# Attention of one decoder step: turns in row halves, other products in 32-column tiles, sample parts added on TensorE, PSUM banks given out freely, a new order

## The chip, the cores and the metric

The kernel runs on one core of one Trainium2 chip. The metric is device time in microseconds (us), median of the runs. One execution is profiled; its span reaches from the first to the last instruction. Engines: TensorE (PE in the profile; PEld is its weight loads), VectorE (DVE), ScalarE (ACT), GpSimd (POOL), and SyncE (SP), which issues nearly all DMAs.

## The reference, cut to what matters

One step of a two-layer decoder for 256 prompt tokens and 8 sample sequences of 4 new tokens each (past 2048), in fp32. Layer 0 is a short convolution, layer 1 is sparse attention; each stands between two half-step SwiGLU FFNs. The change lies in the attention of layer 1 alone. It has 16 heads of 64 (4 key/value heads), and adds three branches:

```
def nsa_attend(q, t_pos, gates, k_cmp, v_cmp, gather_sel, kv_win, s_win):
    s_c = einsum(q, k_cmp) * scale;  p_c = softmax(where(m_c, s_c, NEG)) * m_c;  o_c = einsum(p_c, v_cmp)
    imp = p_c.sum(group).reshape(..., nb_s, ratio).sum(-1)
    score = where(forced, FORCE_BONUS, where(valid, imp, -FORCE_BONUS))
    _, idx = lax.top_k(score, min(TOP_N, nb_s))
    k_sel, v_sel = gather_sel(idx);  p_s = softmax(masked q.k_sel);  o_s = einsum(p_s, v_sel)
    p_w = softmax(masked q.k_win);   o_w = einsum(p_w, v_win)
    return gates[0] * o_c + gates[1] * o_s + gates[2] * o_w
```

## The kernel before, in words

The FFNs and projections are streams of fp32r products, 128x128 weights against 288 token columns. They lie before and behind the attention and the change leaves them alone.

The attention is the function `nsa`. Its last part lays down every piece of work as a step (`step`, a `Task`) with an engine, a duration from the table `TAKES`, the steps it comes after, the buffers it takes (`Slot`, in rings of `RINGS`) and a rank. `Plan.run` lists the steps: of those that can start first it takes the one of the lowest rank, and emits its instructions at once, so the order of each engine's queue is that list. The ranks are the numbers in `CHUNKS`, `HEADS`, `TAILS`, `UNITS` and `COMPRESSED`, found by a search outside the program. `MODES` names the shape in which a step uses TensorE's array ("f" 128x128, "p" 128x64, "c" 128x32 in four column tiles, "h" 64x128 in two row tiles), and the planner counts `SWITCH` for each change of it.

The steps are:

- Samples, `sequences(i)`, four pairs of sequences (32 query rows each for two key/value head pairs, 128 partitions). A head: `small` (scores against compressed and new keys), `max`, `parts` (exp), `share`, `rank`, `best` (the top 16 blocks). Then five chunks of 512 keys, one of the window ("w") and four of the pages: `S` (scores), `top` (mask and maximum, DVE), `exp` (ACT), `turn` (four transposes of 128x128), `copy` (PSUM to SBUF, ACT), `V` (values), and for the first four `og` (the chunk's output to `Og`, ACT). Each chunk has its own maximum, so the parts must be weighted before they are added. The tail: `min`, `wg`, `wg2` (weights `w`), `turn_s`, `copy_s`, `V_s` (the small part), `sum`, `add`, `last`, `own` (weighted sum of the parts and a mask on DVE, into the tile rB or rms), `out` (a product with the 0/1 matrix `Sel` that puts each row in its place) and `oh_s`, `ol_s`.
- Prompt, `prompt_unit(u)`, eight units: `s0`, `s1` (scores of the later and the earlier half of the queries), `t0`, `t1` (DVE) and `e0`, `e1` (ACT), `factor`, `f1`, `f0` (scaling, DVE), three `pturn` of four transposes each, three copies (two on ACT, one on DVE, into PA and PB), `p_v` (ten products), `oh`, `ol`.
- Pages come in through SP: 40 sets of 1 MB, in a fixed order. A set's load is issued by `load_pages` when a `V` step has freed a buffer; the weights of the next stage come behind the last set. Three weight splits (`whi` on ACT, `wlo` on DVE) have the highest ranks and so fill what is left.

PSUM has eight banks of 512 fp32 columns: before, a ring of four ("mm", the scores), one of two ("tr", turns), and one of two ("acc", values and small products).

Of the kernel before, what the change touches and what calls it, by code (L numbers as in the profile page):

```python
# [8 lines left out]
F32 = mybir.dt.float32  # L9
# [44 lines left out]
RINGS = dict(mm=4, tr=2, acc=2, U=2, PA=1, PB=1, S=3, PTs=2, small=2, pc=1, score=1, mk=2, sum=2, PTm=2)  # L54
TAKES = dict(
    small=0.4, max=0.55, parts=0.9, share=0.44, rank=0.21, best=1.5, S=0.87, S2=1.0, top=0.61, top_w=0.89, exp=0.71, turn=0.47, copy=0.5,
    copy_v=0.6, V=0.9, og=0.16, min=0.25, wg=0.38, wg2=1.6, turn_s=0.15, copy_s=0.21, sum=1.57, V_s=0.3, add=0.28, last=0.36, own=0.29,
    out=0.25, oh_s=0.12, ol_s=0.14, cmp=1.34, cmp_e=0.32, cmp_n=2.0, cmp_t=0.28, cmp_c=0.34, s0=0.95, s1=0.54, t0=0.34, t1=0.21, e0=0.49,
    e1=0.385, factor=0.39, f0=1.13, f1=0.6, pturn=0.47, p_v=1.95, oh=0.28, ol=0.34, whi=0.96, wlo_v=1.15, cs=1.2, cs_c=0.5, cs_t=0.5,
# [5 lines left out]
MODES = dict(turn="f", pturn="f", rank="f", turn_s="f", out="f", cmp_t="f", cs="c", cs_t="f", p_v="fp",  # L65
             S="c", V="c", small="c", V_s="c", s0="h", s1="h")
SWITCH = 0.12


NEAR, STAY = 0.129, 56.5102  # L70
CHUNKS = ((964.53, 896.1799), (1327.2414, 995.6261), (1417.341, 1380.5317), (1478.0066, 997.9328),
# [4 lines left out]
HEADS = (952.1558, 1031.7885, 1431.353, 1421.0384)  # L76
TAILS = (1410.3538, 1473.7793, 1457.1762, 926.1094)
UNITS = ((1408.4431, 1368.5397), (1437.9733, 959.7242), (1297.9535, 1272.967), (1420.513, 1500.4049),
    (1413.2876, 1393.186), (1364.7109, 1016.3831), (1045.6014, 1472.1569), (1020.1863, 1529.1656))
COMPRESSED = (1332.6098, 1463.1332)  # L80
SHARED = ("cmp_n", "sum", "share", "own", "wg2", "wlo_v")
# [68 lines left out]
class Plan:  # L150
# [3 lines left out]
    def __init__(self, rings):  # L154
        self.rings = {n: [None] * k for n, k in rings.items()}
        self.free, self.tasks, self.mode, self.port = {}, [], None, (0.0, 0.0)

    def add(self, *a, **k):
        t = Task(*a, **k)
        self.tasks.append(t)  # L160
        return t

    def start(self, t):
# [8 lines left out]
        taken = {}  # L172
        for s in t.slots:
            n = taken[s.ring] = taken.get(s.ring, -1) + 1
            last = self.rings[s.ring][n]
            for x in last.users if last else ():
                if x.end is None:
                    return None
                at = max(at, x.end + (0.0 if x.engine == t.engine else HOP[x.engine]))
        return at  # L180

    def run(self):
        left = list(self.tasks)
        while left:
# [5 lines left out]
            left.remove(t)  # L190
            for s in t.slots:
                self.rings[s.ring] = self.rings[s.ring][1:] + [s]
# [133 lines left out]
def tile_step(ctx, tc, x_turned, state_turned, cmp_pages, sel_pages, cache_win, win_pages, page_table,  # L326
# [9 lines left out]
    banks = {}  # L336

    @contextmanager
    def psum_banks(**counts):
        with tc.tile_pool(name="psum", bufs=2, space=PSUM) as pool:  # L340
            banks.update(pool=pool, **counts)
            yield

    def bank(name):
        return banks["pool"].tile([P, 512], F32, name=name, bufs=banks[name])
# [7 lines left out]
    def accb():  # L353
        return bank("acc")

# [34 lines left out]
    def tr(out, in_):  # L390
        k = in_.shape[0]
        nc.tensor.transpose(out, in_, ident[:k, :k])  # L392

# [509 lines left out]
    def nsa(at):  # L903
# [20 lines left out]
        G, Sel, okvg, okp, vmask = [A(n, [P, w]) for n, w in (("G", P), ("Sel", 64), ("okvg", 16), ("okp", 2), ("vmask", 16))]  # L924
# [39 lines left out]
        put(ts, Sel, lin[:, :64], col["csel"], None, op0=OP.is_equal)  # L964
        put(ts, okvg, lin[:, :16], col["kvg"], None, op0=OP.is_equal)
        put(ts, okp, lin[:, :2], col["kp"], None, op0=OP.is_equal)

# [252 lines left out]


# [51 lines left out]
        cs, cS, turned_ = Slot("acc"), Slot("S"), Slot("tr")  # L1273
# [20 lines left out]
        def cmp_turn():  # L1294
            units["ct"] = trb()
            for a in range(2):
                tr(units["ct"][:, a * P:(a + 1) * P], s[:, a].rearrange("p h n -> p (h n)"))
# [8 lines left out]
        x = Slot("tr")  # L1306
        c4 = step("PE", "cmp_t", cmp_turn, [c3], [x], rank=r)
        cmp_done = step("DVE", "cmp_c", lambda: nc.vector.tensor_copy(PcT, units.pop("ct")[:, :NP]), [c4], uses=[x], rank=r)

        def prompt_unit(u, pr, g):  # L1310

            t, (rs, r) = {}, UNITS[u]
            sl = {n: Slot(n) for n in ("U", "PA", "PB", "acc")}
# [29 lines left out]
            for half in range(2):  # L1343
                banks_ = [Slot("mm"), Slot("mm")]
# [26 lines left out]
            def turn(n):  # L1371
                src_ = (t["S0"], t["S1"][:, :, :P], t["S1"][:, :, P:])[n]
                t["tr", n] = trb()
                for j in range(4):
                    tr(t["tr", n][:, j * P:(j + 1) * P], src_[:, j])

            def put(n):
                if n == 0:
                    t["PA"] = T("PA", [P, 4, NP], F32, RINGS["PA"])
                if n == 2:  # L1380
                    t["PB"] = T("PB", [P, 4, P], F32, RINGS["PB"])
                dst = t["PA"][:, :, n * P:(n + 1) * P] if n < 2 else t["PB"]
                v = t.pop(("tr", n)).rearrange("p (j q) -> p j q", j=4)
                if n == 1:
                    nc.vector.tensor_copy(dst, v)  # L1385
                else:
                    nc.scalar.activation(dst, v, AF.Copy)

            puts = []
            for n in range(3):  # L1390
                x = Slot("tr")
                p = step("PE", "pturn", lambda n=n: turn(n), [(f0, f1, f1)[n]], [x], [sl["U"]], r - 0.2)
                puts.append(step("DVE" if n == 1 else "ACT", "copy_v" if n == 1 else "copy", lambda n=n: put(n), [p] + puts[:1],
                                 {0: [sl["PA"]], 2: [sl["PB"]]}.get(n, []), [x] + [sl["PA"]] * (n == 1), r - 0.2))

            def values():
                o = t["o"] = accb()
                mm(o[:, :NP], VcBig[:, u], PcT, True, False)
                for br in range(2):
                    for a, pt in ((0, t["PA"]), (1, t["PB"])):  # L1400
                        for kp in range(2):
                            vs = V[br + 1][:, a, (2 * pr + kp) * HD:(2 * pr + kp + 1) * HD]
# [358 lines left out]
```

## Time and profile before

| | us |
|---|---|
| median of 3 runs (lowest, highest) | 1186.28 (1185.25, 1186.79) |
| the profiled execution | 1186.15 |
| its span | 1184.1 |
| PE, DVE, ACT, POOL busy over the span | 1172.9, 749.5, 579.8, 171.9 |

The profiled execution lies 2.05 us above its span (what comes before the first and after the last instruction) and 0.13 us below the median. The granted TensorE clock is 0.998 of full speed. Times in the rows below are us from the start of the span; the attention's planned steps run from about 843.5 to 946.8. In the rows, `tr<-ident,S` is a turn, `mm<-...,Qbd` a chunk's scores, `acc<-...,PTs` its values, `mm<-kT,qT` a unit's scores, `acc<-ss,VcBig`, `acc<-PA,V` and `acc<-PB,V` a unit's values. An fp32 product stands there as two instructions, a transpose as one. Instructions that run side by side in tiles of the array overlap in time.

### The profile page before, as it was taken

How to read it: one execution, taken by the hardware profiler on the slowest of the kernel's cores; microseconds unless marked ns; L12 is line 12 of the kernel's file. 1: busy time of each engine (PE TensorE's matmuls, PEld its weight loads, DVE VectorE, ACT ScalarE, POOL GpSimd, SP SyncE). 2: the span in 40 equal slices, each digit the busy share in tenths (PEclk: the TensorE clock that was granted, in tenths of full speed). 3: DMA queues.
4: the chain of work that ended last, by engine and by line, in shares of the span. 5: the costliest groups of instructions: out<-in, count | busy, mean ns of one | idle time of the engine just before them, and what ended most of it. 6: DMA issues, size and time to landing. Idle time of an engine off the chain costs nothing. (4 is left out here: it accounts for less than half of the span.)

```text
span 1184.1 us, 25826 instructions
## 1 busy us (share of the span) xinstructions
PE 1172.9 (99%) x10034; PEld 1114.9 (94%) x10034; DVE 749.5 (63%) x1407; ACT 579.8 (49%) x1013; POOL 171.9 (15%) x221
## 2 busy tenths in 40 slices
PE   9999999999999999999999999999999999999997
PEld 9999999999999999999999999999766799999997
DVE  7663665667766455466564566687688876655654
ACT  6543444534644344445443444544468755434444
POOL 1160111223311100112110011130000021100111
PEclk9999999999999999999999999999999999999999
DMA  7864764766637477467663553597999647765531
GB/s 302 302 206 156 272 196 159 270 212 234 228 134 280 144 241 273 144 191 245 208 230 107 196 196 108 193 367 276 321 374 383 222 162 280 257 224 197 184 114 61
DMA packets 89468, 262.02 MB, mean 221 GB/s; under 512 B 9826, under 2 KB 42979, under 8 KB 74115
## 3 DMA queue, kind: packets, MB, share of 16 engines
q1 hardware_dynamic: 88466, 249.71, 60.2%
q0 software_dynamic: 256, 8.32, 1.9%
q10 hardware_dynamic: 624, 2.34, 0.5%
q8 instruction: 80, 1.31, 0.4%
q14 instruction: 42, 0.34, 0.1%
HBM read 257.31 MB, written 11.35 MB: 227 GB/s over the span
## 5 line engine op out<-in xcount | busy, mean ns | idle before, releaser
L301 DVE TENSOR_TENSOR wlo<-raw,whi 128x1024 fp32r<-128x1024 f32 (+3 forms) x363 | 418.0, 1158 | 229.3 <-ACT whi L291 228.0
L291 ACT ACTIVATE whi<-raw 128x1024 fp32r<-128x1024 f32 (+3 forms) x366 | 345.5, 953 | 191.8 <-PE mm L362 184.4
L362 PE MATMUL mm<-xh,whi 128*128 128x288 f32 x1456 | 419.3, 290 | 0.0
L362 PE MATMUL mm<-xh,wlo 128*128 128x288 f32 x1456 | 416.0, 288 | 0.3 <-DVE wlo L301 0.3
L362 PE MATMUL mm<-xl,whi 128*128 128x288 f32 x1456 | 416.1, 288 | 0.0
L362 PEld LDWEIGHTS mm<-xh,whi 128*128 128x128 f32 x1456 | 271.3, 187 | 1.3 <-issue 0.3
L362 PEld LDWEIGHTS mm<-xh,wlo 128*128 128x128 f32 x1456 | 271.0, 187 | 0.5 <-DVE wlo L301 0.5
L362 PEld LDWEIGHTS mm<-xl,whi 128*128 128x128 f32 x1456 | 271.1, 187 | 0.2
L362 PE MATMUL mm<-Ah,whi 128*128 128x288 f32 x768 | 222.6, 290 | 0.0
L362 PE MATMUL mm<-Al,whi 128*128 128x288 f32 x768 | 221.5, 288 | 0.0
L362 PE MATMUL mm<-Ah,wlo 128*128 128x288 f32 x768 | 221.4, 288 | 0.0
L362 PEld LDWEIGHTS mm<-Ah,whi 128*128 128x128 f32 x768 | 143.7, 187 | 0.5 <-issue 0.4
L362 PEld LDWEIGHTS mm<-Al,whi 128*128 128x128 f32 x768 | 143.8, 187 | 0.0
L362 PEld LDWEIGHTS mm<-Ah,wlo 128*128 128x128 f32 x768 | 143.7, 187 | 0.0
L610 POOL TENSOR_TENSOR a<-s,t 128x288 f32<-128x288 f32 x80 | 66.6, 832 | 520.0 <-DVE t L608 420.5
L606 ACT ACTIVATE s<-t 128x288 f32<-128x288 f32 x88 | 39.0, 444 | 135.4 <-DVE t L604 135.1
L362 PE MATMUL mm<-zh,whi 128*128 128x288 f32 x352 | 101.6, 289 | 0.0
L362 PE MATMUL mm<-zh,wlo 128*128 128x288 f32 x352 | 101.4, 288 | 0.0
L362 PE MATMUL mm<-zl,whi 128*128 128x288 f32 x352 | 101.4, 288 | 0.0
L362 PEld LDWEIGHTS mm<-zl,whi 128*128 128x128 f32 x352 | 65.8, 187 | 0.1
L362 PEld LDWEIGHTS mm<-zh,whi 128*128 128x128 f32 x352 | 65.8, 187 | 0.1
L362 PEld LDWEIGHTS mm<-zh,wlo 128*128 128x128 f32 x352 | 65.8, 187 | 0.0
(314 smaller groups left out, 1096.7 us busy)
## 6 DMA issues: line engine op xcount, KB each, us to landing
raw<-in_w_ffb_gu_dram SPq DMA_DIRECT2D x44, 1024.0 KB, 5.0
raw<-in_w_ffa_gu_dram SPq DMA_DIRECT2D x42, 1024.0 KB, 5.1
cp<-in_cmp_pages_dram SPq DMA_DIRECT2D x256, 128.0 KB, 4.4
early<-in_sel_pages_dram SPq DMA_DIRECT2D x64, 256.0 KB, 5.3
raw<-in_w_ffa_down_dram SPq DMA_DIRECT2D x16, 768.0 KB, 4.2
raw<-in_w_conv_in_dram SPq DMA_DIRECT2D x12, 1024.0 KB, 4.8
raw<-in_w_ffb_down_dram SPq DMA_DIRECT2D x16, 768.0 KB, 4.2
raw<-in_w_ffa_down_dram SPq DMA_DIRECT2D x16, 640.0 KB, 4.0
```

The lines of the kernel that those rows point to most:

```text
L291: self.nc.scalar.activation(parts[0], v, AF.Copy)
L301: (lower or self.nc.vector).tensor_sub(parts[1], v, parts[0])
L362: nc.tensor.matmul(out, lhsT, rhs, start=start, stop=stop, skip_group_check=True)
L606: nc.scalar.activation(s1, t1, AF.Silu)
L610: (nc.vector if last else nc.gpsimd).tensor_mul(a, s1, t2)
```

## The change

1. Turns. `turn`, `pturn` and the turn of the compressed part transpose the upper and lower 64 rows of a block apart (`halves_turned`): each half moves 64 columns instead of 128, in its own row tile of the array and into its own PSUM bank, so a turn holds two banks. The two later `pturn` of a unit become one step, `pturn2`. The tile PT replaces PA and PB.
2. All other products of the plan go in four 32-column tiles (`quarters`): `p_v` (before one 128x128 and eight 128x64 products), `rank`, `out`, and `turn_s`, now a product with the identity. Only one turn (`cs_t`) keeps the 128x128 shape.
3. The samples' parts. `sum`, `add`, `last` and `own` go. `sel` on DVE makes five weighted copies of `Sel` (128x128 each), the small and the last part are copied out of PSUM, and `out` adds six products in PSUM. The products that keep the array at work ahead of the last `out` go from five to three.
4. PSUM is one tile of eight banks. Within the plan, a step takes the banks that come free first; outside it the old three rings are kept.
5. The copies `copy`, `og` and the two new ones go to ACT or DVE by a string of 68 letters, `MOVES`: 49 A, 19 D.
6. New entries in `TAKES`, and new ranks. `STAY` is 3183 (before 56.5): among steps that could start at the same time, one of the array's present shape always goes first.

The core of the diff:

```diff
-RINGS = dict(mm=4, tr=2, acc=2, U=2, PA=1, PB=1, S=3, PTs=2, small=2, pc=1, score=1, mk=2, sum=2, PTm=2)
+RINGS = dict(bank=8, U=2, PT=1, S=3, PTs=2, small=2, pc=1, score=1, mk=2, sum=2, PTm=1, sel=1, last=1)
...
-MODES = dict(turn="f", pturn="f", rank="f", turn_s="f", out="f", cmp_t="f", cs="c", cs_t="f", p_v="fp",
+MODES = dict(turn="h", pturn="h", pturn2="h", rank="c", turn_s="c", out="c", cmp_t="h", cs="c", cs_t="f", p_v="c",
              S="c", V="c", small="c", V_s="c", s0="h", s1="h")
...
+MOVES = "ADDDAAAAAADADAAADDDAAAADADAAAAAAAAAAAAAAAAADDAAAAADDDDAAAAAAAADDAADA"
...
+    def places(self, t):
+        taken = {}
+        for s in t.slots:
+            ring, used = self.rings[s.ring], taken.setdefault(s.ring, [])
+            if s.ring == "bank":
+                used.append(min((self.clear(x, t.engine), n) for n, x in enumerate(ring) if n not in used)[1])
+            else:
+                used.append(len(used))
+        return taken
...
+    def both_banks():
+        a, b = sorted(planned[0].given)
+        return banks[0][:, a:b + 1:b - a]
...
+    def halves_turned(out, in_):
+        for h in range(2):
+            r = slice(h * 64, (h + 1) * 64)
+            nc.tensor.transpose(out[:, h], in_[r], ident[r, r])
+
+    def quarters(out, lhsT, rhs, start=True, stop=True):
+        for q in range(4):
+            c = slice(q * 32, (q + 1) * 32)
+            mm(out[c], lhsT[:, c], rhs, start, stop)
...
                 def turn(d=d):
-                    d["pt"] = trb()
+                    d["pt"] = both_banks()[:, :, :256].rearrange("p h (s x) -> p h s x", s=4)
                     for s in range(4):
-                        tr(d["pt"][:, s * P:(s + 1) * P], d["S"][:, s])
+                        halves_turned(d["pt"][:, :, s], d["S"][:, s])
...
+            def chosen():
+                t["sel"] = [space(k // 2)[:, k % 2 * P:(k % 2 + 1) * P] for k in range(5)]
+                for k in range(5):
+                    ts(t["sel"][k].rearrange("p (h c) -> p h c", h=2), Sel, t["w"][:, 2 + k:3 + k], None, op0=OP.mult)
...
-            def sums():
-                ...
-                ts(a, Og[:, 0], w[:, 2:3], None, op0=OP.mult)
-                for n in range(3):
-                    stt(a, Og[:, 1 + n], w[:, 4 + n:5 + n], a, op0=OP.mult, op1=OP.add)
...
             def turn_out():
                 left_out.append(i)
+                t["o"] = accb()
                 if len(left_out) == 4:
-                    fillers(5)
-                t["o"] = accb()
-                mm(t["o"][:, :64], t["a"], Sel, True, True)
+                    for _ in range(3):
+                        quarters(t["o"][:, P:2 * P], ones, ones)
+                parts_ = [(t["Og"][:, k], t["sel"][k].rearrange("p (h c) -> p h c", h=2)) for k in range(4)]
+                parts_ += [(t["s"], Sel), (t["last"], t["sel"][4].rearrange("p (h c) -> p h c", h=2))]
+                for n, (v, w) in enumerate(parts_):
+                    for q in range(4):
+                        c = slice(q * 32, (q + 1) * 32)
+                        mm(t["o"][c, :64], v[:, c], w[:, q // 2], n == 0, n == 5)
```

More of the change, by code (lines that the diff above doesn't have):

```diff
@@ L50 @@
 WAITS = (24, 3, 4, 9)
-RINGS = dict(mm=4, tr=2, acc=2, U=2, PA=1, PB=1, S=3, PTs=2, small=2, pc=1, score=1, mk=2, sum=2, PTm=2)
+RINGS = dict(bank=8, U=2, PT=1, S=3, PTs=2, small=2, pc=1, score=1, mk=2, sum=2, PTm=1, sel=1, last=1)
 TAKES = dict(
[L56 to L59, printed above, removed]
+    small=0.4, max=0.55, parts=0.9, share=0.44, rank=0.16, best=1.5, S=0.86, S2=1.0, top=0.61, top_w=0.89, exp=0.71, turn=0.25, copy=0.5,
+    copy_v=0.6, og_v=0.2, V=0.875, og=0.16, min=0.25, wg=0.38, wg2=1.6, turn_s=0.22, copy_s=0.21, V_s=0.3, sel=0.68, out=0.75, oh_s=0.12, ol_s=0.14, cmp=1.34, cmp_e=0.32, cmp_n=2.0, cmp_t=0.13, cmp_c=0.34, s0=0.92, s1=0.5, t0=0.34, t1=0.21, e0=0.49,
+    e1=0.385, factor=0.39, f0=1.13, f1=0.6, pturn=0.25, pturn2=0.5, p_v=1.72, oh=0.28, ol=0.34, whi=0.96, wlo_v=1.15, cs=1.2, cs_c=0.5, cs_t=0.5,
     qe=0.75)
@@ L161, in add, with clear @@
         return t
+    def clear(self, last, engine):
+        at = 0.0
+        for x in last.users if last else ():
+            if x.end is None:
+                return INF
+            at = max(at, x.end + (0.0 if x.engine == engine else HOP[x.engine]))
+        return at
+    def places(self, t):
[7 more added lines that the diff above has]
+        return taken
     def start(self, t):
@@ L171, in start @@
             at = max(at, x.end + (0.0 if x.engine == t.engine else HOP[x.engine]))
[L172 to L180, printed above, removed]
+        for name, used in self.places(t).items():
+            at = max(at, *(self.clear(self.rings[name][n], t.engine) for n in used))
+        return None if at == INF else at
     def run(self):
@@ L335, in tile_step @@
     ctx.enter_context(tc.manual_schedule())
[L336 to L342, printed above, removed]
-    def bank(name):
-        return banks["pool"].tile([P, 512], F32, name=name, bufs=banks[name])
+    banks, turns, planned = [], dict(mm=0, tr=0, acc=0), []
+    def bank(name):
+        if planned:
+            n = planned[0].given.pop(0)
+        else:
+            first, count = dict(mm=(0, 4), tr=(4, 2), acc=(6, 2))[name]
+            n, turns[name] = first + turns[name], (turns[name] + 1) % count
+        return banks[0][:, n]
     def mmb():
@@ L1389, in prompt_unit, with turn @@
-            puts = []
-            for n in range(3):
[L1391 to L1394, printed above, removed]
+            def turn(late):
+                src_ = (t["S1"][:, :, :P], t["S1"][:, :, P:]) if late else (t["S0"],)
+                t["tr"] = both_banks()[:, :, :256 * len(src_)].rearrange("p h (n j x) -> p h n j x", n=len(src_), j=4)
+                for n, v in enumerate(src_):
+                    for j in range(4):
+                        halves_turned(t["tr"][:, :, n, j], v[:, j])
@@ L1677, in to @@
         return lambda d: gated(d, v)
-    ctx.enter_context(psum_banks(mm=4, tr=2, acc=2))
+    banks.append(ctx.enter_context(tc.tile_pool(name="psum", bufs=1, space=PSUM)).tile([P, 4096], F32, name="bank").rearrange("p (n c) -> p n c", n=8))
     first = W.load()
```

167 lines of the change are left out of this document (90 added, 77 removed), and 8 rows, old and new, of the table CHUNKS.

## The prediction

> **What bounds the kernel now.** I read the page first, then the engines by stretches, then the chain that ended last within the attention, then single rows. By stretches (engine busy us, number of instructions, clock, DMA share, GB/s):
>
> ```profile
> core 0: us, PE busy (x) PEld busy (x) DVE busy (x) ACT busy (x) POOL busy (x), PEclk, DMA share, GB/s
> 902.00:924.00 22.00, 22.00 (x217) 14.49 (x213) 20.69 (x102) 18.77 (x71) 0.00 (x0) 1.00 0.97 346
> 924.00:947.00 23.00, 22.36 (x321) 16.39 (x321) 19.19 (x72) 16.60 (x48) 0.00 (x0) 1.00 0.55 207
> 843.50:947.00 103.50, 100.60 (x1459) 69.34 (x1460) 87.27 (x415) 79.71 (x275) 0.00 (x0) 1.00 0.90 327
> 947.00:1152.00 205.00, 205.00 (x1612) 204.89 (x1611) 128.00 (x167) 97.79 (x140) 26.47 (x36) 1.00 0.56 202
> ```
>
> Behind the attention PE works 205.00 of 205 us: what the attention saves, the end saves. Inside it (843.5 to 946.8, 103.2 us) PE is busy 100.60, but DVE 87.27 and ACT 79.71 are close behind, and from 902 to 924 DVE has 20.69 of 22. The chain (start, duration, group of instructions):
>
> ```profile
> 843.71 0.40 PE acc L357 x13
> ...
> 900.58 1.02 PE tr L392 x8
> 901.60 1.06 PE mm L357 x8
> 902.66 2.08 PE acc L357 x18
> 904.75 1.02 PE tr L392 x8
> 905.77 0.65 PE mm L357 x8
> 906.41 0.59 PE tr L392 x4
> 907.00 1.85 PE mm L357 x16
> ...
> 913.67 1.01 PE acc L357 x32
> 914.68 1.02 PE tr L392 x8
> 915.70 1.51 PE mm L357 x16
> ...
> 931.46 1.88 PE acc L357 x64
> ...
> 942.41 1.38 PE tr L357 x10
> ...
> 945.90 0.87 PE tr L357 x6
> 946.76 30.44 PE mm L362 x240
> ```
>
> From about 876 on the chain is PE behind PE, nearly without a gap. The same rows give prices. Eight turns take 1.02 and four 0.59, so a block of 128x128 costs (1.02 - 0.59)/4 = 0.108, and 0.16 is left for entering the shape. Two values steps in a row take 1.88, two apart 2 x 1.01: 0.14 for entering theirs. A unit's `s0` and `s1` in a row take 1.51, apart 1.06 + 0.65: 0.20. So a change of the array's shape costs 0.14 to 0.20; I take 0.16. By the shape in each row of the timeline there are 77 groups from 843.71 to 945.90: 76 changes, 12.2 us.
>
> **The change, part by part.**
>
> Turns in halves. Twenty chunks with 4 blocks and eight units with 12 make 176 blocks (two more in the compressed part). Whether a half is worth half depends on the weight loads, which these rows show (first two windows of weight loads, then groups):
>
> ```profile
> 893.17 0.20 PEld L392 LDWEIGHTS tr<-ident,S 128*128 128x128 f32 x2 [0.87 <-ACT S L1500]
> 893.17 0.31 PEld L392 LDWEIGHTS tr<-ident,S 128*128 128x128 f32 x3 [0.87 <-ACT S L1500]
> 893.75 0.19 PEld L357 LDWEIGHTS mm<-kT,qT 64*128 64x128 f32 x2 [0.17 <-issue]
> L392 PEld LDWEIGHTS tr<-ident,S 128*128 128x128 f32 x180 | 19.2, 141 | 9.7 <-issue 4.0 <-ACT S L1500 2.5 <-ACT sq L1576 0.8
> L357 PEld LDWEIGHTS mm<-kT,qT 64*128 64x128 f32 x128 | 9.9, 186 | 2.3 <-issue 1.4 <-DVE sm L1357 0.2 <-DVE fg L1564 0.2
> ```
>
> One load for a turn takes 0.141 and two together 0.20, so the second began 0.06 behind the first; only the third comes 0.11 later, when it must wait for a product. Two loads of 64-row tiles, 0.186 each, end together in 0.19: row tiles load side by side. Their products do too: the group of eight that takes 0.65 would take 8 x 0.108 = 0.86 one after the other. So two halves, side by side, each with 64 of 128 columns, should cost 0.054 a block: 178 x 0.054 = 9.6 us less on PE. The ends: nothing, if a half still costs 0.108; 12.5, if the loads let go of more.
>
> The Trainium skill ("TensorE: Matmul & The Clock Gate", section LDWEIGHTS) speaks against this: a load's time goes with its 128 columns, about 107 ns, and not with its rows, so a half would load as long as a whole. By that rule this term would be 0; the 0.06 between two loads above disagrees for transposes, and the measurement decides.
>
> Shapes. Turns and unit scores now share the 64-row shape and all else the 32-column shape. With the groups in the order of before, 56 changes would be left of 76: 20 x 0.16 = 3.2 us. A new order that clings to the shape may save up to 20 more; one pulled about by the copies, nothing: 0 to 6.4, I take 3.2. The columns of `p_v` stay: a row of the 128x32 shape costs 1.01 - 0.16 = 0.85 for 512 columns, so its 256 + 2 x (256 + 128) = 1024 cost 1.70, and before it was 2.08 less two entries, 1.76.
>
> Added on PE. `out` becomes six products of 64 columns, 0.85/8 = 0.11 each, instead of one: 4 x 0.55 = 2.2. `turn_s` as a product 4 x 0.11 = 0.4. Two of the five filling products go, 1.38/5 each with the entry: about -0.45. Net 2.2. Sum on PE: 9.6 + 3.2 - 2.2 = 10.6 us less, 92.6 for the stage with all the waits it has.
>
> DVE and ACT. The rows (busy, mean ns of one; the same set stands there a second time with rB for rms, in all 9.2 us):
>
> ```profile
> L1583 DVE SCALAR_TENSOR_TENSOR rms<-Og,wg,rms 128x128 f32<-128x128 f32 x6 | 2.1, 352 | 0.3
> L1595 DVE SCALAR_TENSOR_TENSOR rms<-acc,wg,rms 128x128 f32<-128x128 f32 x2 | 0.7, 351 | 0.8 <-PE acc L357 0.8
> L1591 DVE TENSOR_TENSOR rms<-acc,rms 128x128 f32<-128x128 f32 x2 | 0.6, 292 | 0.2
> L1599 DVE TENSOR_TENSOR rms<-rms,okp 128x128 f32<-128x128 f32 x2 | 0.6, 289 | 0.0
> L1581 DVE TENSOR_SCALAR rms<-Og,wg 128x128 f32<-128x128 f32 x2 | 0.6, 276 | 0.0
> L1365 DVE TENSOR_SCALAR S<-S,sm 128x256 f32<-128x256 f32 x32 | 9.1, 348 | 0.0
> L1385 DVE COPY PA<-tr 128x512 f32<-128x512 f32 x8 | 5.5, 686 | 1.6 <-PE tr L392 1.6
> L1509 ACT ACTIVATE PTs<-tr 128x512 f32<-128x512 f32 x20 | 11.6, 590 | 2.0 <-PE tr L392 1.9
> L1527 ACT ACTIVATE Og<-acc 128x128 f32<-128x128 f32 x16 | 4.3, 270 | 2.0 <-PE acc L357 1.8
> ```
>
> DVE loses 9.2. It gains 20 weighted copies of `Sel`: alone such a one takes 0.28, back to back 32 of twice the length take 9.1, so 0.14 to 0.28; they stand in fives, so near the lower end: 0.17, 3.4. The string gives DVE eight unit copies (as before), two chunk copies (2 x 0.69) and nine short ones (seven `og`, two last parts; 0.2 to 0.29, I take 0.25): 3.6. So DVE goes to 85.1, a gain of only 2.2 (0.5 to 3). ACT loses two chunk copies and seven `og`, gains six short ones: 79.7 - 1.5 = 78.2, not a bound. The copies read two banks with a step; no row shows that, and I take the price of one bank, with 0 to 0.1 more for each of 44, mostly beside PE. DVE then has 85.1 of PE's 92.6 us, so where it is late, PE has less other work to cover it.
>
> Pages. SP issues each load when values free a buffer, so a new order moves them:
>
> ```profile
> DMA  9999998999999999999999999999999999999992
> L1084 SPq DMA_DIRECT2D early<-in_sel_pages_dram x16: 332/333/477, 908.3 to 918.7; - x16
> DMA to landing us min/median/max: 4.1/4.9/5.3
> ```
>
> From 843.5 to 924 the DMA engines are full (first row, forty slices, nines but for the last). The last page is issued at 918.7 and lands at 918.7 + 5 = 923.7; a faster PE can't bring it earlier. Behind it come that chunk's S 0.85, top and exp (512 columns each, so about as long as the 512-column copy on DVE) 0.7 each, turn 0.4, copy 0.6, V 1.0, last copy 0.3, `out` 0.8 and `oh_s` 0.3, and for the eight hand-overs between engines I allow 0.2 each: 7.3, say 8 us. The floor is 932 against 946.8, a gain of 14.8 at most. The weights behind the pages are hidden by the stretch to 1152, where the DMA share is 0.56.
>
> PSUM as one tile costs outside the attention nothing: its rings are the same and PE has no gap up to 1152; if that cover were gone, I would allow 0.5.
>
> Sum: PE alone gives 92.6. With DVE at 85.1 and the pages at 88.5, three bounds lie within 7.5 us, and waits that one covered for the other now show; I add 2.4 and take 95.0, 8.2 less than 103.2. Against the profiled execution: 1186.15 - 8.2 = 1177.95, and the median lay 0.13 above it: 1178.1, said as 1178.0. About 2.4 us (0.2%) is what a measurement can tell from no change.
>
> **The rivals.**
>
> - DVE ends it. DVE was idle 103.5 - 87.27 = 16.2 us of the stage. If those waits (scores, exps, start and end) stay, the stage is 85.1 + 16.2 = 101.3, a gain of 2 to 4: 1182.5. For it: 20.69 of 22. Against it: in the chain DVE seldom stands, so much of its idle time is waiting for PE.
> - Halves cost as much as wholes (weights pace them). Then 10.6 - 9.6 = 1.0 is left on PE: 1185.1. Against it: the 0.06 above. The Trainium skill's section on LDWEIGHTS in "TensorE: Matmul & The Clock Gate" would lead here.
> - The pages end it: the new order leaves as much behind 923.7 as now (23 us). The gain is gone: 1185 to 1186. Against it: the prompt's units need no page and can fill the time before.
> - The slow side: a turn waits for two banks. PE takes its queue in order, so a turn that waits for the second bank holds all scores and values behind it. There are 20 + 16 = 36 such steps. At 0.23 us more for each the 8.2 is gone, from 0.3 on the kernel is slower by over 0.2%, and at 0.4 it ends at 1186.15 + 14.4 - 8.2 = 1192. For it: a bank is held until its copy is done, 0.6 to 0.7 behind each turn, and scores and values now compete for the same eight. Against it, the waits of before with a ring of only two:
>
> ```profile
> PEld tr L392 <- ACT PTs L1509: 0.2, 1, 0.2
> PEld tr L392 <- ACT PB L1387: 0.3, 1, 0.3
> ```
>
>   The Trainium skill ("TensorEngine Tiling (Array Packing)", Restrictions and Gotchas) says the same of the price: row tiling raises PSUM pressure, since different row tiles write to different banks. No run of before shows it.
> - More than forecast: the new order reaches the floor of the pages, 932: 1172.
>
> **How the numbers follow.** Chances: the forecast 0.56, with its own range 1174.5 to 1181; DVE 0.17; halves as wholes 0.06; pages 0.05; banks 0.08; the floor 0.08. Faster by over 0.2% are the forecast, the floor and most of DVE's: 0.79. Within 0.2%: the rest of DVE's, halves as wholes, pages: 0.12. Slower: banks and a little of the pages: 0.09. The range from 1172.5 to 1185.0 leaves out the banks, half of the floor, and part of the pages: under 0.2.
>
> **What would show it.** Right: eight halves (four blocks) in about 0.22 us plus the entry; fewer than 60 groups of one shape; DVE near 85 and ACT near 78 in the stage; the first product of the output projection near 938.5; the last page still landing near 924. Wrong: weight loads of halves 0.1 apart; turns with waits on copies of over 0.2 us; DVE with idle time of over 13 us while PE waits for it; or DMA slices before 924 that are not full, which would mean that buffers come free too late and the pages themselves come later.

## The result, and the profile after

| | us (lowest, highest) | against before |
|---|---|---|
| before, in the same sessions | 1185.76 (1184.91, 1186.79) | |
| the changed kernel | 1192.88 (1191.01, 1194.25) | 1.0059 [1.0041, 1.0076] |
| predicted | 1178.0 (1172.5, 1185.0) | |

The change made the kernel slower, by 7 us, and the forecast was wrong in sign and outside its range. The profiled execution took 1192.68 us, 2.08 over its span.

In the rows of the new kernels every PSUM tile is called `bank`. `bank<-ident,S` is a turn; L423 (L431 or L424 in the variants) is the helper of the half turns, L382 (L390, L383) that of the products, and L387 (L395, L388) is the output projection behind the attention.

Engines by stretches, the changed kernel (the first two answer to the stretches of before, the third is its whole stage):

```profile
902.00:924.00 22.00, 20.35 (x493) 15.30 (x489) 17.68 (x98) 17.84 (x66) 0.00 (x0) 1.00 0.99 351
924.00:947.00 23.00, 18.35 (x448) 13.48 (x439) 19.50 (x82) 17.34 (x58) 0.00 (x0) 1.00 0.60 234
843.50:953.30 109.80, 94.93 (x2070) 69.85 (x2071) 87.74 (x421) 79.68 (x272) 0.00 (x0) 0.98 0.88 313
953.00:1158.00 205.00, 205.00 (x1612) 204.89 (x1611) 127.80 (x167) 97.02 (x138) 26.21 (x35) 1.00 0.55 201
```

Behind the attention nothing changed (205.00 of 205). Inside it PE, which before was idle for 0 of 22 and 0.64 of 23 us, is now idle for 1.65 and 4.65. The chain that ended last:

```profile
858.75 0.46 PE bank L423 x8
...
903.42 0.70 PE bank L423 x16
...
915.15 0.89 PE bank L423 x24
...
953.26 30.42 PE bank L387 x240
```

Two things stand here. The output projection begins at 953.26, not at 946.76: the stage (from 843.9) grew from 103.2 to 109.4 us. And one more half costs what was forecast: from 8 to 24 half turns the group grows by 0.43, 0.027 a half, 0.054 a block. Entering the shape costs more than forecast: 8 x 0.027 of the 0.46 are the halves, so 0.24 is left, not 0.16. PE's work in the stage fell, from 100.60 to 94.93 us, and PE waits. For what, the list of waits says. These are the rows on the tile PTs, which the copy of a turn writes (who waited for it: us, times), first of the changed kernel, then of before:

```profile
who waited for it (us, times):
  PEld bank L382: 6.0, 9
  PEld bank L423: 5.0, 7
  PE bank L423: 3.7, 6
...
  PE bank L382: 2.6, 4
  DVE Og L1271: 2.4, 2
  DVE S L1556: 1.8, 1
```

```profile
who waited for it (us, times):
  PEld acc L357: 2.0, 4
...
  PEld tr L392: 0.4, 2
  PE acc L357: 0.2, 1
```

The four rows of PE and its loads add up to 17.3 us, where the three of before add up to 2.6. (A load and a product can wait over the same stretch, so the sum counts some time twice: PE as a whole was idle for 14.9 us of the stage.) Some rows make no sense as data flow: `S L1556` is a mask and maximum on scores and takes nothing from PTs. Nor does this copy of a chunk's output:

```profile
861.68 0.29 DVE L1271 COPY Og<-bank 128x128 f32<-128x128 f32 x1 [1.64 <-ACT PTs L1269]
```

The built program gives the reason. `both_banks` hands a turn two banks of the one PSUM tile as a slice with a step, `[:, a:b + 1:b - a]`. The copy that empties them is recorded as reading everything from bank a to bank b. In the changed program that range alone makes 46 waits of the attention name a later instruction than their own banks ask for; in before it makes none. Of the 53 steps that take two banks, 8 have neighbours, and 29 are emptied by one copy of both. Reads wait for reads too, in 26 of the 46: nine copies and seven masks on DVE wait so for a copy on ACT. The Trainium skill ("PSUM — Partial Sum Buffer", section on PSUM bank collisions) says that two engines on one bank need a dependency, reads and writes alike. The wait of 1.64 us above is of that kind, except that the two copies share no bank: the one's bank only lies between the other's two.

### The profile page after: what moved, and what is told of

The parts are those of the page before. It is cut to its first block, busy times and chain, and to the rows that moved or that the text cites. A ratio compares the mean times of both kernels' runs of the same rounds, so it can differ in the third digit from the quotient of the medians.

```text
span 1190.6 us, 27007 instructions
## 1 busy us (share of the span) xinstructions
PE 1167.7 (98%) x10646; PEld 1115.6 (94%) x10646; DVE 749.2 (63%) x1411; ACT 579.6 (49%) x1010; POOL 171.8 (14%) x221
## 3 DMA queue, kind: packets, MB, share of 16 engines
q8 instruction: 84, 1.38, 0.5%
## 4 chain that ended last, share of the span: by engine, by line
PE 95%; DVE 2%; DMA 1%; ACT 1%; issue 0%; SPq 0%; DVEq 0%; ACTq 0%
PE bank L387 83%; PE bank L382 11%; DMA early<-in_win_pages_dram 1%; PE bank L423 1%; DMA wlo<-in_sel_pages_dram 1%; ACT PTs L1269 0%; DVE S L1556 0%; PE bank L417 0%; ACT S L1395 0%; DVE PT L1271 0%; ACT PT L1269 0%; DVE S L1420 0%; DVE S L1391 0%; DVE PTs L1271 0%; DVE S L1417 0%
## 5 line engine op out<-in xcount | busy, mean ns | idle before, releaser
L387 PE MATMUL bank<-xh,whi 128*128 128x288 f32 x1472 | 424.1, 290 | 0.0
L387 PE MATMUL bank<-xh,wlo 128*128 128x288 f32 x1472 | 420.8, 288 | 0.3 <-DVE wlo L322 0.3
L387 PE MATMUL bank<-xl,whi 128*128 128x288 f32 x1472 | 420.7, 288 | 0.0
L387 PEld LDWEIGHTS bank<-xh,whi 128*128 128x128 f32 x1472 | 274.2, 187 | 1.4 <-issue 0.3
L387 PEld LDWEIGHTS bank<-xh,wlo 128*128 128x128 f32 x1472 | 274.0, 187 | 0.7 <-DVE wlo L322 0.7
L387 PEld LDWEIGHTS bank<-xl,whi 128*128 128x128 f32 x1472 | 274.1, 187 | 0.3
L387 PE MATMUL bank<-Ah,whi 128*128 128x288 f32 x768 | 222.6, 290 | 0.0
L387 PE MATMUL bank<-Al,whi 128*128 128x288 f32 x768 | 221.5, 288 | 0.0
L387 PE MATMUL bank<-Ah,wlo 128*128 128x288 f32 x768 | 221.4, 288 | 0.0
L387 PEld LDWEIGHTS bank<-Ah,whi 128*128 128x128 f32 x768 | 143.7, 187 | 0.5 <-issue 0.4
L387 PEld LDWEIGHTS bank<-Al,whi 128*128 128x128 f32 x768 | 143.8, 187 | 0.0
L387 PEld LDWEIGHTS bank<-Ah,wlo 128*128 128x128 f32 x768 | 143.7, 187 | 0.0
L387 PE MATMUL bank<-zh,whi 128*128 128x288 f32 x352 | 101.6, 289 | 0.0
L387 PE MATMUL bank<-zh,wlo 128*128 128x288 f32 x352 | 101.4, 288 | 0.0
L387 PE MATMUL bank<-zl,whi 128*128 128x288 f32 x352 | 101.4, 288 | 0.0
L387 PEld LDWEIGHTS bank<-zl,whi 128*128 128x128 f32 x352 | 65.8, 187 | 0.1
L387 PEld LDWEIGHTS bank<-zh,whi 128*128 128x128 f32 x352 | 65.8, 187 | 0.1
L387 PEld LDWEIGHTS bank<-zh,wlo 128*128 128x128 f32 x352 | 65.8, 187 | 0.0
```

The costliest lines, as they stand in the source:

```text
L387: nc.tensor.matmul(out, lhsT, rhs, start=start, stop=stop, skip_group_check=True)
```

## The experiments

**Where the banks lie.** Theory A: these stretched waits cost the gain. Rivals: B, the order that clings to the array's shape (among steps that could start at the same time, one that keeps the shape goes first); C, too few banks for turns that hold two. Four kernels, all with the changed kernel's steps.

`adjacent` keeps the order, and gives a step of two banks neighbours where it can (41 of 53):

```diff
+            late = [max(0.0, self.clear(x, t.engine) - at) for x in self.real]
+            if len(asked_) == 2:
+                self.given = list(min((max(late[a], late[b]) + 0.2 * (b - a - 1), a, b) for b in range(8) for a in range(b))[1:])
```

> The changed kernel with the same order of every engine; only the physical banks differ: a turn takes two neighbouring banks where they are free. Theory A (stretched waits): a copy that reads two banks a step apart is tracked as if it read all banks between them, so instructions on those banks wait for it and it for them. Counted in the built programs, 46 waits of the attention name a later instruction than the bank needs; before the change none, here 7. A expects the stage to fall from 109.4 us to 94 to 99, and the time to 1176 to 1182. Theory B (order): the long stretches of one array shape put PE behind copies, whichever banks: no change, 1191 to 1194. Theory C (too few banks, two held by each turn): as many banks are held as long, so no change, 1191 to 1194.

`split` keeps the banks too, and copies each with an instruction of its own:

```diff
-                o = to()
+                o, v = to(), from_()
+                for o, v in [(o[:, h], v[:, h]) for h in range(2)] if both else [(o, v)]:
```

> The changed kernel with the same order and the same banks, but each copy that reads two banks is two copies of one bank each (29 steps, so 29 more copies on ACT and DVE). No stretched wait is left. A expects 1178 to 1186 (the gain of neighbouring banks less 29 x 0.1 to 0.3 us on two engines). B and C expect it no faster, or slower by the added copies: 1192 to 1198.

`whole` keeps order and banks, but turns whole blocks into the first bank of the two:

```diff
-                    d["pt"] = both_banks()[:, :, :256].rearrange("p h (s x) -> p h s x", s=4)
+                    d["pt"] = banks[0][:, min(planned[0].given)].rearrange("p (s x) -> p s x", s=4)
                     for s in range(4):
-                        halves_turned(d["pt"][:, :, s], d["S"][:, s])
+                        tr(d["pt"][:, s], d["S"][:, s])
```

> The changed kernel with the same order and the same two banks held by each turn, but the turns are whole 128x128 blocks again, each into one bank, so no copy reads two banks. PE has 178 x 0.054 = 9.6 us more and some 30 changes of shape more. A expects the lost waits to pay for most of that: 1186 to 1193. B and C expect the added PE work on top of the waits: 1197 to 1204.

`loose` is `adjacent` without the clinging (`NEAR, STAY = 0.0, 0.0`):

> Neighbouring banks as in the first kernel, but the order no longer clings to the array's shape (STAY 0 instead of 3183; same ranks). The plan itself counts 8 us more for this order. A expects it 4 to 9 us slower than the kernel with neighbouring banks alone, 1182 to 1189. B expects it faster than that kernel, below 1188 where that one stays above 1191.

Measured: adjacent 1184.86 (ratio to before 0.9990 [0.9979, 1.0002]), split 1184.57 (0.9996 [0.9985, 1.0008]), whole 1183.76 (0.9985 [0.9976, 0.9995]), loose 1189.4 (one run). Stretched waits left in the built programs: 7, 0, 0. Who waited for PTs in adjacent:

```profile
  PEld bank L431: 1.2, 5
  PEld bank L390: 0.9, 2
...
  PE bank L431: 0.2, 1
```

2.3 us in place of 17.3, and 8.0 us less time; split, with other means and the old banks, gives 8.3. Theory A holds for that part. C falls as its cause (the turns of adjacent and split still hold two banks). B as a whole falls too: without the clinging the one run of loose was slower. But A expected 1176 to 1182 of adjacent, and adjacent got before's time. And `whole`, whose turns keep PE busy for 24.3 us where those of split take 18.4, was not slower at all (A expected 1186 to 1193). Something else was eating the gain.

**TensorE's instructions.** The longest waits of PE in adjacent are for nothing that the profile shows (us, times, longest); the chain near the end reads:

```profile
PE bank L390 <- issue: 4.4, 2, 2.7
```

```profile
934.04 4.92 PE bank L390 x161
938.97 2.74 issue
941.71 4.27 PE bank L390 x36
945.98 4.07 PE bank L395 x32
```

2.74 us of nothing, on the path, in the middle of a unit's values. The queue of instruction transfers has 84 packets and 1.38 MB, 16 KB each, for 21,614 records of PE (products, weight loads, waits), 257 a packet; before has 80 packets for 20,427. So 256 instructions come in one packet, 64 bytes each (that size is also what the Trainium skill gives, "Perfetto Trace Analysis", The 4-stage abstract model). I counted PE's records from the first one on and took, from 820 us on, every gap of over 0.25 us whose instruction waits for no semaphore:

```
kernel      gap at us (length)                                     record number modulo 256
after       948.92 (0.55)                                          193
adjacent    905.06 (1.62), 938.97 (2.74)                           193, 193
split       882.36 (1.43), 905.36 (1.83), 929.33 (1.30), 941.57 (1.15)   193 each
whole       905.25 (0.97)                                          193
before      none
```

In the 17 kernels of this document there are 29 such gaps, in 13 of them, and all 29 stand at record 193 of a block: PE has run out of instructions. The packets agree: in all 29 PE goes on 2.2 to 2.9 us behind the start of a packet, and each time that packet started only after PE had begun the block before. In adjacent PE began the blocks before the two gaps at 901.37 and 935.52, the packets started at 904.48 and 939.41, and PE went on at 906.68 and 941.71. Halves and quarters are more and shorter records (about 4200 in the stage, 3000 in before; whole has 8% fewer than adjacent), so a block lasts a shorter time. `bursts` and `bursts2` measure it by itself, in before, with products that nothing reads:

```diff
+    def burst(groups, w):
+        p = accb()
+        for _ in range(groups):
+            for q in range(4):
+                c = slice(q * 32, (q + 1) * 32)
+                mm(p[c, :w], ones[:, c], xT[:, 0, :w], True, True)
...
+        burst(192, P)                 # bursts: ahead of plan.run()
...
+        burst(192, P)                 # bursts: behind the last product
+        burst(96, 2 * P)
...
+        for b in range(NB):           # bursts2: behind the last product
+            nc.scalar.dma_start(win_s[b], cache_win[0, b, NT:])
+        burst(384, P)
+        burst(192, P)
```

> The kernel before, with three runs of extra products that nothing reads: 192 groups of four products of 32 columns over 128 values just ahead of the attention stage (transfers of pages run), the same 192 groups behind the last product of the kernel (few transfers left), and then 96 groups of four over 256 values. In the traces so far a group over 128 values goes through twice in 0.22 us with 16 records (8 products, 8 weight loads), 73 records a us, and a group over 256 values in 0.43 us, 37 records a us. Theory D (TensorE's instructions come in blocks of 256, one packet of 16 KB each, and a block comes too late where more than some 180 are issued within the 4.1 us behind the start of its packet): both runs over 128 values show idle gaps of 1 to 2 us on TensorE with no wait, about one for 512 records, five or six in each, and last 48 to 53 us instead of 42; the run over 256 values shows none. If the gaps come from full DMA engines alone, only the first run has them. If D is wrong, none has them and both last 42 us.

Measured: the first run begins at 843.07 and has one long gap, 2.23 us at 854.35, some 780 records behind its beginning; the pages had kept the DMA engines full until then (share 0.97 to 1.00). Behind it, with these idle, it has two gaps of 0.31; the second run, with the DMA engines idle, has two of 0.32; the run over 256 values has none. So the first form of theory D (blocks always 4 us under way) was wrong: with idle DMA engines 73 records a us are kept up nearly without a gap.

> The kernel before, with the eight 1 MB copies of the window cache moved from the last layer to its end, and right behind their issue 576 groups of four products of 32 columns over 128 values that nothing reads (about 126 us of TensorE at 0.22 us a group, 73 records a us). For some 25 to 50 us the copies keep the 16 DMA engines busy, then these are idle. Theory D in its mended form (blocks of 256 instructions arrive later when the DMA engines are full): idle gaps of 1 to 2.5 us, one for 512 to 1024 records, while the copies run, and gaps of at most 0.4 us behind them, as in the quiet run of bursts. If full DMA engines do not matter: gaps of at most 0.4 us throughout.

Engines by stretches of bursts2 (the columns before the last two are the clock and the DMA share):

```profile
1185.00:1195.00 10.00, 6.20 (x197) 5.81 (x189) 0.00 (x0) 0.00 (x0) 0.00 (x0) 0.84 1.00 329
1195.00:1201.80 6.80, 5.64 (x128) 4.95 (x128) 0.00 (x0) 0.00 (x0) 0.00 (x0) 0.62 1.01 324
1201.80:1205.90 4.10, 0.00 (x0) 0.00 (x0) 0.00 (x0) 0.00 (x0) 0.00 (x0) 1.00 0.54 213
1215.00:1225.00 10.00, 10.00 (x376) 9.98 (x368) 0.00 (x0) 0.00 (x0) 0.00 (x0) 1.00 0.02 3
```

While the copies keep the DMA engines full, PE stops for 4.94 us at 1191.20 and for 4.13 at 1201.78, exactly 256 records apart; the copies end at 1205.4, PE goes on at 1205.91, and in the 120 us behind that no such gap is over 0.32. (The share counts a packet in the stretch in which it starts; those under way fill the engines until 1205, so the 0.54 is too low.) The gaps were longer and came sooner than I expected (1 to 2.5 us, one for 512 records or more). What is late is the start of the packet: 6.4 and 7.4 us behind PE's first record of the block before in these two gaps, 1.2 to 1.7 us where the DMA engines are idle, 2.2 to 4.0 us at the gaps of the attention. Full DMA engines make a block late.

What this costs the changed order is measured by asking for fewer records. `fewer` is adjacent with 64-column products in `p_v` and whole filling products:

```diff
-                        for q in range(4):
-                            kp, c = q // 2, pr * P + q * 32
-                            mm(o[q * 32:(q + 1) * 32, a * P:NP], V[br + 1][:, a, c:c + 32],
+                        for kp in range(2):
+                            c = pr * P + kp * 64
+                            mm(o[kp * 64:(kp + 1) * 64, a * P:NP], V[br + 1][:, a, c:c + 64],
```

> adjacent, with fewer and no larger work for TensorE: the prompt units' value products in 64 columns instead of 32 (4 for 8), and the fillers as whole products; some 300 of 4280 records of the stage less, just where the two long gaps without a wait stood (1.6 us at 905 and 2.7 us at 939), but two more changes of shape a unit, 8 units, 0.16 us each, 2.6 us. Theory D (late instruction blocks cost adjacent 4 us on its chain): both gaps go, 1181 to 1184 us against 1184.9 for adjacent. Theory E (VectorE and ScalarE set the end) and theory P (the pages set it): the gaps are covered anyway, 1184.5 to 1187.

Measured: 1183.09, 0.9975 [0.9966, 0.9984]; one long gap (1.97 us at 902.57) in place of two, none near the end, where the projection now begins at 943.33. The time is the one D expected, 1.8 us under adjacent, though only one of the two gaps went; the intervals of the two ratios still touch, so the size is uncertain. `tight` also halves the products of `out` and gives 50 of 53 steps neighbours; `tightwhole` is tight with the whole turns of above:

> fewer, with the output products of the samples in 64 columns as well (12 for 24, four times, just the group in which fewer still waited 2.0 us at 902.6 without a cause that the trace names), and with neighbouring banks for 50 of the 53 steps of two banks (41 in adjacent and fewer). Theory A (stretched waits) with theory D (late instruction blocks): both rests go, 1180 to 1182.5 us against 1183.1 for fewer. If neither rest is on the way to the end: 1182.5 to 1184.

> tight, with whole turns in one bank instead of halves in two; nothing else differs. This prices the halves when the stretched waits and most late blocks are gone: 176 blocks of 0.054 us, 9.6 us of TensorE's work by the prediction's term. If TensorE's work sets the stage: 3 to 9 us slower than tight. If the order and the hand-overs set it (theory P or E, or what the plan can't see): within 1.5 us of tight.

Measured: tight 1183.32, 0.9975 [0.9963, 0.9986], no better than fewer, so the two rests are not on the way to the end; tightwhole 1184.93, 0.9993 [0.9983, 1.0002], with no late block at all. The turns of the two (busy us and mean ns; tight has 0.7 us more in four turns that stay whole):

```profile
L431 PE MATMUL bank<-ident,S 64*128 64x64 f32 x352 | 17.3, 229 | 2.5 <-ACT S L1568 0.8 <-DVE PT L1279 0.5 <-DVE PTs L1279 0.5
L425 PE MATMUL bank<-ident,S 128*128 128x128 f32 x180 | 24.9, 280 | 0.9 <-DVE PTs L1279 0.2 <-ACT PTs L1277 0.2 <-ACT S L1568 0.2
```

The halves take 6.9 us off PE, and with stretched waits and most late blocks gone this is worth 1.6 us (2.1 by the ratios), far from the 3 to 9 expected if PE's work set the stage. So it sets little of it.

**VectorE.** `light` is adjacent without three of the four scalings in `f0` (they are not computed), 6.3 us less on DVE:

```diff
-                    for n in range(4):
-                        ts(S[:, n], S[:, n], t["sm"][:, n:n + 1], None, op0=OP.mult)
+                    ts(S[:, 0], S[:, 0], t["sm"][:, 0:1], None, op0=OP.mult)
```

> adjacent, with three of the four scalings of each prompt unit's first scores left out (they are not computed): 24 operations of 0.26 us, 6.3 us less on VectorE, on the path of each unit. Theory E (VectorE sets the end): 1178 to 1180.5 us. Theories D and P: 1183 to 1185.5, at most the 2 us that lie on the way of the last units.

Measured: 1183.92, 0.9988 [0.9974, 1.0001], 0.9 us under adjacent, which is no difference clear of noise, and far from the 1178 to 1180.5 of theory E (VectorE sets the end). DVE's work does not set it either.

**Pages.** In all kernels with the new order the last page lands late: 929.3 in the changed kernel, 928.8 in adjacent, 928.3 in tight, 926.3 to 927.5 in the others, against 923.7 before. Three kernels load 2 MB more ahead of the stage, by moving two of the window cache's copies there from the last layer (issued at 832.6), which sets the pages back by 4 to 5 us: `morepages` (adjacent), `beforepages` (before), `tightpages` (tight):

```diff
                 pages[key] = load_chunk(t, b, j)
                 rings[key] = ring
+                if n in (20, 26):
+                    b = (n - 20) // 6
+                    nc.gpsimd.dma_start(win_s[b], cache_win[0, b, NT:])
...
-        for b in range(NB):
+        for b in range(2, NB):
```

> adjacent, with two of the eight 1 MB copies of the window cache moved from the last layer into the stretch in which the pages load, 5 to 6 us of the 16 DMA engines' time by the rate of 360 GB/s there; nothing else changes. The last page of adjacent lands at 928.8 us, 17 us ahead of the stage's end, and that of before at 923.7. Theory P (the last page's landing sets the end): the last page lands near 934 and the time is 1189 to 1191 us. Theories D and E: the pages come later, but the steps that need them come later still, 1184 to 1187 us.

> The kernel before, with the same two 1 MB copies of the window cache moved ahead of the attention stage as in morepages (there they were issued at 832.6 us, and every page from 842 on came 4 to 5 us later, the last one at 932.8 instead of 928.8; the time was about 3 us over adjacent). In before the stage ends 23 us behind its last page, in adjacent 17. If the new order leaves less room between the pages and the end than the old one (theory P): the last page lands near 928 and the time rises by less than 1.5 us, 1185 to 1187.5. If late pages cost the same in any order, 1188 to 1190.5.

> tight, the best of the variants with the changed kernel's order (stretched waits and most late blocks gone), with the same two copies moved. Theory P (with those gone the pages set the end, so each us of page time counts nearly in full): the last page near 932 and 1186.5 to 1188.5, 3 to 5 us over tight. If TensorE's or VectorE's queues set the end: 1183 to 1185.

| | last page | time | ratio to before | over its own kernel |
|---|---|---|---|---|
| morepages | 932.8 (928.8) | 1187.97 | 1.0025 [1.0013, 1.0038] | 3.1 |
| beforepages | 927.9 (923.7) | 1188.92 | 1.0026 [1.0016, 1.0035] | 3.1 |
| tightpages | 932.8 (928.3) | 1186.86 | 1.0008 [0.9999, 1.0017] | 3.5 |

The last column compares medians; by the ratios it is 4.2, 3.1 and 3.9. The same delay costs about the same in the old order (the second of the two outcomes named for beforepages), and tightpages lies where theory P (the last page sets the end) had it, morepages between the two ranges. By the medians each us of page costs about 0.75 us of time, although the stage ends 15 to 24 us behind its last page. So the new order's pages, 4.6 us late in tight and 5.6 in the changed kernel, should cost it some 3.5 to 4 us by this estimate. It is rough: fewer's last page lands 2 us before tight's, and the two take the same time. Why are the pages late? The first `exp` on ACT and the first turn on PE, in before and then in the changed kernel (start, duration):

```profile
848.84 0.19 ACT L1500 ACTIVATION_READ_ACCUMULATOR S<-S,nb 128x1 f32 x1
849.13 0.63 PE L392 MATMUL tr<-ident,S 128*128 128x128 f32 x4 [0.97 <-issue]
```

```profile
848.71 2.02 PE L382 MATMUL bank<-early,Qbd 128*32 128x512 f32 x16
849.66 0.20 ACT L1560 ACTIVATION_READ_ACCUMULATOR S<-S,nb 128x1 f32 x1
...
850.58 0.41 PE L382 MATMUL bank<-whi,Qbd 128*32 128x256 f32 x2
...
850.70 0.63 PE L382 MATMUL bank<-whi,Qbd 128*32 128x256 f32 x6
851.01 0.75 PE L382 MATMUL bank<-wlo,Qbd 128*32 128x256 f32 x8
851.44 1.18 PE L382 MATMUL bank<-early,Qbd 128*32 128x512 f32 x8
852.55 0.46 PE L423 MATMUL bank<-ident,S 64*128 64x64 f32 x8
```

Before turns 0.1 us behind the exp. The new order turns 2.7 us behind it: scores of four later chunks have the array's present shape, a turn would start a `SWITCH` later, and with `NEAR` 0 only a step that can start first is looked at. The first values step, which frees the first page buffer, so comes at 853.7 instead of 851.4, and the DMA engines are less full meanwhile (before, then the changed kernel; DMA share is the last but one column):

```profile
852.00:856.00 4.00, 4.00 (x72) 2.98 (x66) 3.74 (x26) 4.00 (x18) 0.00 (x0) 1.00 0.92 288
```

```profile
852.00:856.00 4.00, 3.89 (x66) 2.20 (x60) 3.25 (x12) 2.31 (x6) 0.00 (x0) 1.00 0.68 223
```

`searched` has tight's products, neighbouring banks chosen by the planner itself, and ranks and copy engines searched anew by the planner's own count. `early` is the same with one rule more and a search with that rule:

```diff
+            near, stay = (NEAR, STAY) if first >= 12 else (0.3, 0.0)
```

> The changed kernel with tight's products (64 columns in the units' values and the samples' outputs), with the planner choosing neighbouring pairs of banks itself (not afterwards), and with ranks and copy engines searched anew for that by the planner's own count: it ends its stage at 93.6 us, the order of the changed kernel at 92.6 with the banks free. adjacent lost 9.9 us against its plan on the chip, fewer 7.2. If what is lost comes from banks and blocks that the plan did not know (A and D), this order loses 4 to 6 us: 1179 to 1182. If it comes from the hand-overs in general, it loses 7 to 10 as well: 1183 to 1187.

> searched, but in the first 12 us of the plan a step that changes the array's shape may go first (the window of choice is 0.3 us there and clinging to the shape costs nothing), with ranks searched anew for that. In the plan the first turn starts at 6.1 instead of 9.8 us and the first values step ends at 8.5 instead of 13.1, so the first page buffer comes free 3 to 4.6 us earlier; the plan's end is 95.0 instead of 93.6. Theory P with its cause (the order clings to the shape, so the first values step and with it all pages come late): the engines of the DMA have no dip between 852 and 856 us, the last page lands 1.5 to 3 us before that of searched (928.4), and the time is that of searched or up to 2 us less, 1181 to 1184, although the plan is 1.4 us longer. If the late first values step does not move the pages: the last page near 928 and 1184 to 1187.

Measured: searched 1184.10 (1181.20 to 1185.09), 0.9974 [0.9964, 0.9983]. Its times spread with the granted clock (the five up to 1182.39 have 0.998 or 0.999, the six from 1184.10 have 0.995 to 0.997), so the ratio, about 1182.9, and the median differ, and which of its two expectations holds stays open. early 1179.94 (1179.29 to 1180.86), 0.9948 [0.9935, 0.9962], better than I expected and the fastest of all. The stretches and the chain of early:

```profile
852.00:856.00 4.00, 3.50 (x60) 1.93 (x56) 3.85 (x15) 3.65 (x13) 0.00 (x0) 1.00 1.00 345
924.00:947.00 23.00, 21.42 (x345) 17.43 (x344) 16.44 (x61) 14.71 (x42) 0.00 (x0) 1.00 0.70 260
```

```profile
941.47 30.43 PE bank L388 x240
```

The dip is gone (1.00), the last page lands at 924.9, there is no late block, and the projection begins at 941.47. Against its plan of 95.0 us the stage ends about 2 us late; that of adjacent ended 9.9 late. The plan is 1.4 us longer than that of searched, and the kernel is 3.1 us faster by the ratios, 4.2 by the medians. The search also moved other steps, so not all of this is shown to be the pages'.

## Why the prediction was wrong

The step that failed first is the term for the copies that "read two banks with a step". It stood in the sum at the price of one bank, with 0 to 0.1 us more for each and mostly beside PE. The copy's own time was as said (0.60 us for 512 columns, 0.59 before); what it made others wait for was not in the sum, and the runs put 8.0 us on it. Without these waits (adjacent) the change is level with before, neither slower nor clearly faster. The second step that failed is the pages, "a faster PE can't bring it earlier": it asked whether the last page could come sooner than 923.7, and not whether the new order would bring it later, which it did by 5.6 us.

The forecast was 14.9 us too low. By the medians the runs divide this so: 8.0 for stretched waits (changed kernel to adjacent), 1.8 for late instruction blocks (adjacent to fewer, near the noise), 1.0 the other way (fewer to searched, another order), 4.2 for the order's late first turn and late pages (searched to early, 3.1 by the ratios, with the reservation above). The last 1.9, from early down to the forecast, stay open. Point by point:

- Turns in halves: the price of a half was right (0.027), that of entering was not (0.24 for 0.16), so the turns took 6.5 us off PE and not 9.6: 25.6 us for 180 blocks in before, in the changed kernel the first row here and 0.7 in four turns that stay whole.

```profile
L423 PE MATMUL bank<-ident,S 64*128 64x64 f32 x352 | 18.4, 230 | 8.4 <-ACT PTs L1269 2.4 <-DVE PT L1271 1.7 <-ACT S L1560 1.3
L423 PEld LDWEIGHTS bank<-ident,S 64*128 64x128 f32 x352 | 14.3, 138 | 15.7 <-issue 3.5 <-ACT PTs L1269 3.4 <-ACT S L1560 1.9
```

  The rival that the weights pace them falls, though its premise holds. The load of a half takes 0.138 us where that of a whole took 0.141. So the rule of the Trainium skill ("TensorE: Matmul & The Clock Gate", section LDWEIGHTS) that columns count and rows do not holds here. But the loads of two halves run side by side, so a pair is through in 0.054.
- Its worth was wrong too: the prediction made PE's work the stage's time one for one, and tight and tightwhole give 1.6 to 2.1 us for 6.9. PE without a gap was read as PE the bound; beforepages shows that late pages cost the same stage time as well.
- Shapes: 56 changes forecast, 30 in the changed kernel. More than the 3.2 us should then have left PE's work, but it fell by 5.7 us in all (100.60 to 94.93, at a clock of 0.98), where the sum had 10.6; no run prices the changes alone. The prediction asked what clinging saves and not what it puts off: the first turn, and with it all the pages.
- DVE and ACT: 85.1 us were forecast for DVE, and adjacent has 85.9 from 843.5 to 945. That DVE might end it, the rival with 0.17, falls by light.
- Pages: the part on what would show it named the DMA slices that are not full; 0.68 where 0.92 was is that sign.
- The copies: the sum counted 44 with two banks, but the 16 behind the later turns of the units read one bank each. The waits come from 29.
- The slow rival, two banks to a turn, gave 1192 and the time came out at 1192.9, but not for its reason, so that it fits is luck. Holding a bank until its copy is done is not what cost it: split holds them as long and is 8.3 us faster. Spread over its 36 steps the 8.0 us are 0.22 each, just its break-even; the rest came from blocks and pages, which were not in its sum.
- The allowance of 2.4 us for waits that come to light was a guess: early's whole loss against its plan is about 2 us, and the changed kernel's about 17 (109.4 us against a plan of 92.6).

## What to carry to other kernels

Where two buffers lie in one tile, look at what the program records for a copy with a step: the span between them counts, so give pairs neighbours or copy each by itself. When a change makes instructions shorter and more, look at how long PE takes for 256 records while the DMA engines are full: at the gaps of this stage the next block was there 4.5 to 6.4 us after PE had begun the one before, and a PE that is done sooner runs dry. And follow the first step that frees a load's buffer: what is put off there comes back at the end of a saturated stream, even where the last transfer seems to land long before the end.

## What the runs showed of the hardware

- TensorE's instructions come in packets of 256. PE could go on 2.2 to 2.9 us behind the start of a packet in all 29 gaps, and a packet starts late when data fills the DMA engines: with these full a stop was up to 4.9 us long (bursts2), with these idle never over 0.32.
- PE's stops can also cost clock. In adjacent, behind the 2.74 us:

```profile
938.90:941.70 2.80, 0.07 (x2) 0.00 (x0) 2.47 (x4) 0.14 (x2) 0.00 (x0) 0.94 0.52 111
941.70:944.00 2.30, 2.29 (x28) 1.51 (x32) 0.00 (x0) 0.00 (x0) 0.00 (x0) 0.50 0.80 338
944.00:946.00 2.00, 2.00 (x24) 1.33 (x17) 0.42 (x1) 0.83 (x2) 0.00 (x0) 0.81 0.16 61
```

  The granted clock is 0.50 when PE starts again, and back within 4 us; the 36 products there took 4.27 us, where the same 36 in light, behind a stop of 1.08, took 2.79. The Trainium skill ("TensorE: Matmul & The Clock Gate", What's actually happening) puts the fall behind an idle window of about 3.4 us; here a stop of 2.74 was enough. The length of one stop does not decide it: behind 2.23 us in bursts the clock stayed at 1.00, and in the changed kernel it fell to 0.50 behind stops of 0.58 and 0.74 us only.

```profile
855.90:859.30 3.40, 2.09 (x30) 0.95 (x28) 2.46 (x9) 1.52 (x4) 0.00 (x0) 1.00 0.82 261
859.30:862.70 3.40, 3.40 (x72) 3.39 (x68) 1.00 (x3) 0.69 (x3) 0.00 (x0) 0.50 1.01 313
```

  What decides it, no run here separates.
